# RMS norm with repeated rows: one store cut in two, and a load that waits for its first part

## The chip, the cores and the metric

The kernel runs on one core of a Trainium2 chip. The metric is the device time of one execution in microseconds (us); lower is better. Before the change it is 238.33 us, the median of 3 runs (238.19 to 238.34).

## The reference: what is computed

The input `x` has 8 x 512 rows of 2048 float32 values, `gamma` has 2048. Each row is divided by its root mean square, multiplied by `gamma`, and written twice, one copy after the other:

```python
x_rep = np.repeat(x, 2, axis=1)
rms = np.sqrt((x_rep ** 2).mean(axis=-1, keepdims=True) + 1e-6)
return ((x_rep / rms) * gamma[None, None, :]).astype(np.float32)
```

So 33.6 MB are read and 67.1 MB written. The arithmetic is done once for each input row, not once for each output row.

## The kernel before: tiles, stages and order

**The buffer.** One tile `y` fills most of the on-chip memory: 128 partitions, each with 24 rows of 2048 float32 (8 KB a row). The code names three groups of eight rows by their first row: `first` = 0, `second` = 8, `third` = 16. A load brings eight input rows to every partition (64 KB a partition, 8.39 MB in all). Four loads make the whole input, L0 to L3 here. Every load gives two stores, each of four input rows doubled to eight output rows, so also 64 KB a partition and 8.39 MB. There are eight stores, written here as S00 and S01 (from L0), S10 and S11 (from L1), and so on. In `out_t` a partition's 64 KB of a store are contiguous in device memory.

**Two groups.** The function `four(n, ...)` handles loads `n` and `n + 1` and their four stores, and is called with `n` = 0 and `n` = 2. Inside it:

- Load `n` goes to rows 4 to 11 (`first + K`), load `n + 1` to rows 16 to 23 (`third`).
- Rows 4 to 7 are normalised into rows 0, 2, 4, 6 and copied into 1, 3, 5, 7; these eight are store (n, 0).
- Rows 8 to 11 are normalised, last row first, into 14, 12, 10, 8, and copied to the odd rows; store (n, 1).
- Rows 16 to 19 go into rows 0 to 7, once store (n, 0) has read them: store (n + 1, 0).
- Rows 20 to 23 go into rows 16 to 23: store (n + 1, 1).

So L2, the first load of the second group, writes rows 4 to 11 and may start only when S01 (rows 8 to 15) and S10 (rows 0 to 7) have been read out. L3 writes rows 16 to 23 and waits for S11.

**The engines.** `squares` runs on ScalarE (ACT): a square with a sum for each row, then a square root over the sums. `scale` runs on VectorE (DVE): a reciprocal, then for each row one operation that multiplies by the reciprocal and by `gamma_b`. `repeat` makes the second copy of the rows, on ACT or DVE. The order on every engine is the order of the code (`manual_schedule`); waits are put in by the framework wherever two accesses touch the same bytes of `y`.

**The queues.** All loads and stores are issued by SyncE (SP) and go through one DMA queue, in order: L0, L1, S00, S01, S10, S11, L2, L3, S20, S21, S30, S31. Each is carried by 16 DMA engines, 8 partitions to an engine. SP waits in order too: while it waits to issue L2 it can't issue L3. `gamma` comes through ACT's DMA queue in `constants()`, one large DMA and `E` small ones of 16 values, into rows 0 to 2 of `y` on partition 0. GpSimd (POOL) then spreads them to all partitions in two `partition_broadcast` operations (L132 and L136). POOL does nothing else but four small fills at the start.

The lines that matter below are L50 (issue of a load), L53 (issue of a store), L63, L67 (`squares`), L73, L75 (`scale`), L82 (`repeat`), and L122 to L136 (`constants`).

Of the kernel before, what the change touches and what calls it, by code (L numbers as in the profile page):

```python
# [1 line left out]

# [4 lines left out]


@with_exitstack
def kernel(  # L10
    ctx: ExitStack,
    tc: tile.TileContext,
    x: bass.AP,
    gamma: bass.AP,
    out: bass.AP,
):
    nc = tc.nc
    P = nc.NUM_PARTITIONS
    f32 = mybir.dt.float32
    Act = mybir.ActivationFunctionType  # L20
    Alu = mybir.AluOpType

    B, S, D = x.shape
    Bo, So, Do = out.shape
    R = So // S
    assert R == 2 and D == Do and B == Bo and So == S * R
    eps = 1e-6
    inv_d = 1.0 / float(D)


    K = 4
    N = B * S
    ntiles = N // (P * K)
    assert N % (P * K) == 0 and ntiles == 8
    H = 2
    x_t = x.rearrange("b s d -> (b s) d").rearrange("(n p k) d -> n p k d", p=P, k=H * K)
    out_t = out.rearrange("b s d -> (b s) d").rearrange("(n p h j) d -> n h p (j d)", p=P, h=H, j=K * R)

    singles = ctx.enter_context(tc.tile_pool(name="singles", bufs=1))
    rows = ctx.enter_context(tc.tile_pool(name="rows", bufs=1))  # L40
    junk = ctx.enter_context(tc.tile_pool(name="junk", bufs=1, space=bass.MemoryType.PSUM))
    small = ctx.enter_context(tc.tile_pool(name="small", bufs=4))

    y = rows.tile([P, 3 * K * R, D], f32, name="y")
    first, second, third = 0, K * R, 2 * K * R

    def load(n, at):
        nc.sync.dma_start(out=y[:, at : at + H * K, :], in_=x_t[n])  # L50

    def store(n, h, to):
        nc.sync.dma_start(  # L53
            out=out_t[n, h], in_=y[:, to : to + K * R, :].rearrange("p j d -> p (j d)")
        )

    def squares(at, rows):

        n = len(rows)
        ss = small.tile([P, n], f32, name=f"ss{n}")  # L60
        for c, k in enumerate(rows):
            sq = junk.tile([P, D], f32, name="sq")
            nc.scalar.activation(  # L63
                out=sq[:], in_=y[:, at + k, :], func=Act.Square, accum_out=ss[:, c : c + 1]
            )
        rms = small.tile([P, n], f32, name=f"rms{n}")
        nc.scalar.activation(out=rms[:], in_=ss[:], func=Act.Sqrt, scale=inv_d, bias=eps_t[:])  # L67
        return rms

    def scale(at, to, rows, rms):  # L70
        n = len(rows)
        rstd = small.tile([P, n], f32, name=f"rstd{n}")
        nc.vector.reciprocal(out=rstd[:], in_=rms[:])  # L73
        for c, k in enumerate(rows):
            nc.vector.scalar_tensor_tensor(  # L75
                out=y[:, to + R * k, :], in0=y[:, at + k, :], scalar=rstd[:, c : c + 1],
                in1=gamma_b[:], op0=Alu.mult, op1=Alu.mult,
            )

    def repeat(to, k0, k1, copy):  # L80
        y_r = y[:, to + R * k0 : to + R * k1, :].rearrange("p (k r) d -> p k r d", r=R)
        copy(out=y_r[:, :, 1, :], in_=y_r[:, :, 0, :])  # L82

    ctx.enter_context(tc.manual_schedule())

    half = K // 2
    up, down = list(range(K)), list(range(K - 1, -1, -1))

    def four(n, constants, step):


        load(n, first + K)
        constants()
        load(n + 1, third)
        for rows in (up[:half], up[half:]):
            scale(first + K, first, rows, squares(first + K, rows))
        repeat(first, 0, half, nc.scalar.copy)
        repeat(first, half, K, nc.vector.tensor_copy)
        store(n, 0, first)
        scale(second, second, down, squares(second, down))  # L100
        repeat(second, half, K, nc.scalar.copy)
        for k in range(0, half, step):
            repeat(second, k, k + step, nc.vector.tensor_copy)
        store(n, 1, second)
        roots = [squares(third + h * K, up) for h in range(H)]
        scale(third, first, up, roots[0])
        repeat(first, 0, half, nc.scalar.copy)
        repeat(first, half, K, nc.scalar.copy)
        store(n + 1, 0, first)
        scale(third + K, third, up, roots[1])  # L110
        repeat(third, 0, K, nc.scalar.copy)
        store(n + 1, 1, third)

    gamma_b = singles.tile([P, D], f32, name="gamma_b")
    G, E = 16, 3
    C = D // G - E
    gamma_s = y[0:1, 0:2, :].rearrange("p k (c d) -> p (k c) d", c=G // 2)
    gamma_t = y[0:1, 2, :]
    eps_t = singles.tile([P, 1], f32, name="eps_t")

    def constants():
        nc.scalar.dma_start(  # L122
            out=gamma_s[0:1, :, :C],
            in_=gamma[: G * C].rearrange("(p c d) -> p c d", p=1, c=G),
        )
        for c in range(E):
            at = G * C + c * G
            nc.scalar.dma_start(
                out=gamma_t[0:1, c * G : (c + 1) * G],
                in_=gamma[at : at + G].partition_broadcast(1),  # L130
            )
        nc.gpsimd.partition_broadcast(  # L132
            out_ap=gamma_b[:, : G * C].rearrange("p (c d) -> p c d", c=G),
            in_ap=gamma_s[0:1, :, :C],
        )
        nc.gpsimd.partition_broadcast(out_ap=gamma_b[:, G * C :], in_ap=gamma_t[0:1, : E * G])  # L136
        nc.vector.memset(eps_t, eps)  # L137

        root = singles.tile([P, 1], f32, name="root")[:]
        nc.scalar.activation(out=root, in_=eps_t[:], func=Act.Sqrt)  # L140

    four(0, constants, half)
    four(2, lambda: None, 1)


# [1 line left out]
_INS = ['x', 'gamma']  # L147
_OUTS = [((8, 1024, 2048), 'float32')]


# [23 lines left out]
```

## Time and profile before

| | |
|---|---|
| median of 3 runs | 238.33 us |
| the profiled execution's own time | 238.07 us |
| its span (first to last instruction) | 236.2 us |
| DVE busy | 84.5 us (36%) |
| ACT busy | 110.2 us (47%) |
| POOL busy | 2.8 us (1%) |
| moved by DMA | 100.68 MB, 426 GB/s over the span |
| GpSimd's broadcast L132 starts, takes | 10.65, 2.24 us |
| GpSimd's broadcast L136 starts, takes | 23.01, 0.32 us |

The profile shows one execution. Times of single events count from the start of its span. An engine's busy time has no waiting in it. A DMA has two times: when its queue's engine issued it, and when it landed, that is when its completion was signalled. Between the two it can stand in the queue behind other transfers. The time outside the span (238.07 less 236.2) is the launch and the end of the program.

### The profile page before, as it was taken

To read this page: it belongs to the slowest core of one execution; us is meant where nothing else is said; L and a number is where in the kernel's file an instruction comes from. 1 tells how busy PE (TensorE), PEld (TensorE's weight loads), DVE (VectorE), ACT (ScalarE), POOL (GpSimd) and SP (SyncE) were. 2 spreads that over 40 slices of the span, in tenths; PEclk is the share of its full clock that TensorE was granted. 3 is DMA by queue.
4 is the path that set the end of the run, shared out by engine and by line. 5 is a ranking of instruction groups with operands and counts; after the bars stand their busy time and mean duration, and the time that the engine had idled before them with its cause. 6 is when DMAs were issued, how large, how long until landed. Compare 5 with 4: busy or idle time off the path is not lost.

```text
span 236.2 us, 226 instructions
## 1 busy us (share of the span) xinstructions
DVE 84.5 (36%) x48; ACT 110.2 (47%) x86; POOL 2.8 (1%) x6
## 2 busy tenths in 40 slices
DVE  0000396594699500000000007928919992000000
ACT  2001989479998470000000049991999957400000
POOL 0110000000000000000000000000000000000000
DMA  9898989989898989989898998989898998989894
GB/s 355 356 533 355 510 377 422 466 366 522 355 533 356 533 355 422 466 377 510 355 533 355 488 400 355 533 355 533 355 533 355 488 399 355 533 355 533 355 533 178
DMA packets 1767, 100.68 MB, mean 426 GB/s; under 512 B 230, under 2 KB 230, under 8 KB 230
## 3 DMA queue, kind: packets, MB, share of 16 engines
q1 hardware_dynamic: 1728, 100.66, 98.7%
q10 hardware_dynamic: 38, 0.01, 0.0%
q14 instruction: 1, 0.01, 0.0%
HBM read 33.56 MB, written 67.11 MB: 426 GB/s over the span
## 4 chain that ended last, share of the span: by engine, by line
DMA 45%; ACT 26%; DVE 12%; issue 2%; DVEq 0%
DMA y<-in_x_dram 26%; DMA out_dram<-y 20%; ACT sq L63 15%; DVE y L75 12%; ACT y L82 11%; ACT rms L67 1%; DVE rstd L73 0%; DVEq L75 0%
## 5 line engine op out<-in xcount | busy, mean ns | idle before, releaser
L63 ACT ACTIVATE sq<-y 128x2048 f32<-128x2048 f32 x32 | 60.1, 1878 | 71.1 <-DMA y<-in_x_dram 70.4
L75 DVE SCALAR_TENSOR_TENSOR y<-y,rstd,gamma_b 128x2048 f32<-128x2048 f32 x32 | 73.8, 2349 | 1.6 <-DMA out_dram<-y 1.0
L82 ACT COPY y<-y 128x4096 f32<-128x4096 f32 (+1 forms) x10 | 42.6, 4283 | 19.1 <-DVE y L75 18.3
L73 DVE RECIPROCAL rstd<-rms 128x4 f32<-128x4 f32 (+1 forms) x10 | 1.7, 170 | 109.2 <-ACT rms L67 109.2
L82 DVE COPY y<-y 128x4096 f32<-128x4096 f32 (+1 forms) x5 | 9.2, 1865 | 0.1
L63 ACT ACTIVATION_READ_ACCUMULATOR sq<-y 128x1 f32 x32 | 6.0, 186 | 0.0
L67 ACT ACTIVATE rms<-ss,eps_t 128x4 f32<-128x4 f32 (+1 forms) x10 | 3.0, 297 | 0.3
L140 ACT ACT_TABLE_LOAD x1 | 1.3, 1283 | 2.6 <-issue 2.6
L132 POOL PARTITION_BROADCAST gamma_b<-y x1 | 2.2, 2243 | 10.2 <-DMA y<-in_gamma_dram 10.2
L136 POOL PARTITION_BROADCAST gamma_b<-y x1 | 0.3, 323 | 10.1 <-DMA y<-in_gamma_dram 10.1
L137 DVE MEMSET eps_t<- 128x1 f32 x1 | 0.1, 59 | 0.8 <-PEq L158 0.8
L140 ACT ACTIVATE root<-eps_t 128x1 f32<-128x1 f32 x1 | 0.2, 203 | 0.0
L158 POOL MEMSET const-bfloat16-1.0<- 128x1 bf16 x1 | 0.1, 102 | 0.0
L158 POOL MEMSET const-float32-0.0<- 128x1 f32 x1 | 0.1, 99 | 0.2 <-issue 0.2
L158 POOL MEMSET const-uint8-127<- 128x1 uint8 x1 | 0.1, 101 | 0.0
L158 POOL MEMSET const-float32-1.0<- 128x1 f32 x1 | 0.1, 98 | 0.0
## 6 DMA issues: line engine op xcount, KB each, us to landing
out_dram<-y SPq DMA_DIRECT2D x8, 24.8
y<-in_x_dram SPq DMA_DIRECT2D x4, 31.4
y<-in_gamma_dram ACTq DMA_DIRECT2D x3, 0.1 KB
y<-in_gamma_dram ACTq DMA_DIRECT2D x1, 7.8 KB, 9.8
```

The costliest lines, as they stand in the source:

```text
L63: nc.scalar.activation(out=sq[:], in_=y[:, at + k, :], func=Act.Square, accum_out=ss[:, c : c + 1])
L67: nc.scalar.activation(out=rms[:], in_=ss[:], func=Act.Sqrt, scale=inv_d, bias=eps_t[:])
L73: nc.vector.reciprocal(out=rstd[:], in_=rms[:])
L75: nc.vector.scalar_tensor_tensor(out=y[:, to + R * k, :], in0=y[:, at + k, :], scalar=rstd[:, c : c + 1], in1=gamma_b[:], op0=Alu.mult, op ...
L82: copy(out=y_r[:, :, 1, :], in_=y_r[:, :, 0, :])
L132: nc.gpsimd.partition_broadcast(out_ap=gamma_b[:, : G * C].rearrange("p (c d) -> p c d", c=G), in_ap=gamma_s[0:1, :, :C],)
L136: nc.gpsimd.partition_broadcast(out_ap=gamma_b[:, G * C :], in_ap=gamma_t[0:1, : E * G])
L137: nc.vector.memset(eps_t, eps)
L140: nc.scalar.activation(out=root, in_=eps_t[:], func=Act.Sqrt)
L158: nc = _bacc.Bacc("TRN2", target_bir_lowering=False, num_devices=1)
```

## The change

Three edits. The last store of the first group, S11, is issued as two DMAs, one of seven rows of 8 KB in every partition and one of the eighth row. Between the two groups GpSimd copies one element, from row 4 to row 16 of partition 0. It writes a byte range that the seven-row DMA reads, so it waits for that DMA to land. It reads a byte range that L2 will write, so L2 waits for the copy. And `gamma` is cut differently: 2016 values in the large DMA and two small ones of 16 (before 2000 and three). A fourth, small edit: in the second group the two rows' copy on DVE before S21 is one operation and not two. The number of DMAs on both queues together stays 16.

```diff
-    def store(n, h, to):
-        nc.sync.dma_start(
-            out=out_t[n, h], in_=y[:, to : to + K * R, :].rearrange("p j d -> p (j d)")
-        )
+    def store(n, h, to, cuts=()):
+        rows = y[:, to : to + K * R, :].rearrange("p j d -> p (j d)")
+        ends = [c * D for c in (0, *cuts, K * R)]
+        for c0, c1 in zip(ends, ends[1:]):
+            nc.sync.dma_start(out=out_t[n, h][:, c0:c1], in_=rows[:, c0:c1])
...
-    def four(n, constants, step):
+    def four(n, constants, cuts=()):
...
-        for k in range(0, half, step):
-            repeat(second, k, k + step, nc.vector.tensor_copy)
+        repeat(second, 0, half, nc.vector.tensor_copy)
         store(n, 1, second)
...
-        store(n + 1, 1, third)
+        store(n + 1, 1, third, cuts)
...
-    G, E = 16, 3
+    G, E = 16, 2
...
-    four(0, constants, half)
-    four(2, lambda: None, 1)
+    four(0, constants, (K * R - 1,))
+    nc.gpsimd.tensor_copy(out=y[0:1, third, 0:1], in_=y[0:1, first + K, 0:1])
+    four(2, lambda: None)
```

In the built program the copy on GpSimd stands after its two broadcasts. Its own queue waits first for L0, then for L1 and the seven-row DMA, then for ACT. On SP the order becomes L0, L1, S00, S01, S10, S11's seven rows, S11's one row, L2 (which waits for S00, S01, S10 and the copy), L3 (which waits for both parts of S11), and the four stores of the second group.

## The prediction

> **What bounds the kernel now.** I read the page's busy times first, then its DMA queues.
>
> ```profile
> DVE 84.5 (36%) x48; ACT 110.2 (47%) x86; POOL 2.8 (1%) x6
> q1 hardware_dynamic: 1728, 100.66, 98.7%
> ```
>
> No engine is near its span. The one queue that carries all loads and stores keeps the 16 DMA engines busy for 98.7% of it. The kernel is a train of 12 equal transfers, and only what leaves a hole in that train or makes it longer costs time. The chain that ended last, in order of time, gives the train's marks (start, duration, what):
>
> ```profile
> 0.72 21.92 DMA y<-in_x_dram
> ...
> 76.17 23.86 DMA out_dram<-y
> 100.03 0.02 issue
> 100.04 38.78 DMA y<-in_x_dram
> 138.82 0.02 issue
> ...
> 155.30 22.23 DMA out_dram<-y
> ```
>
> Landings: L0 at 22.64, S10 at 100.03, L2 at 138.82, S20 at 177.53. From L0 to S10 there are four transfers, 77.39 us, 19.35 each. From L2 to S20 two, 38.71, again 19.35. From S10 to L2 two (S11 and L2), 38.79, so 0.09 more than 2 x 19.35: the hand-over from stores to loads costs about 0.09 today, with L2 queued long before. L0, which found idle engines, took 21.92 from issue to landing, 2.57 more than 19.35. These two numbers, 0.09 for a load already in the queue and 2.57 for a load that has to start the engines, are what the forecast turns on.
>
> The timeline around the change:
>
> ```profile
> 80.04 7.02 ACT L82 COPY y<-y 128x8192 f32<-128x8192 f32 x1 [3.90 <-DVE y L75]
> 87.08 0.33 SPq L53 DMA_DIRECT2D out_dram<-y  x1
> 100.04 20.04 SPq L50 DMA_DIRECT2D y<-in_x_dram  x2
> 138.85 1.88 ACT L63 ACTIVATE sq<-y 128x2048 f32<-128x2048 f32 x1 [51.79 <-DMA y<-in_x_dram]
> ```
>
> S11 is issued at 87.08 and lands at 119.73: the second L50 issue is released by it. L2 is issued at 100.04, so it stands in the queue for the whole 19 us of S11. No compute runs between 87.06 and 138.85; ACT and DVE wait for L2 and nothing else.
>
> **The change, part by part.**
>
> *The new wait, on the path.* L2's issue moves from 100.04 to after the seven rows' landing and the copy.
>
> 1. Seven rows land. S11 starts when S10 ends, landing to landing: 100.03 + 7/8 x 19.35 = 116.96.
> 2. GpSimd wakes. The same engine waited for small DMAs twice:
>
> ```profile
> 0.33 0.10 POOL L158 MEMSET const-uint8-127<- 128x1 uint8 x1
> 10.65 2.24 POOL L132 PARTITION_BROADCAST gamma_b<-y  x1 [10.22 <-DMA y<-in_gamma_dram]
> 23.01 0.32 POOL L136 PARTITION_BROADCAST gamma_b<-y  x1 [10.12 <-DMA y<-in_gamma_dram]
> ```
>
> The first followed its DMA's landing by 0.08 (landing 10.57 in the trace's records of completions). The second, which like the copy has a separate wait instruction ahead of it (43 ns on POOL's queue), followed by 0.18 (landing 22.83). I take 0.18, because the copy has two such waits, of which the second is the late one; 0.08 is the lower end.
> 3. The copy of one element. No such operation is in the trace. The fill of 128x1 takes 0.10 and reads nothing; the 48-column broadcast takes 0.32 and also moves data across partitions; the 2000-column one, 2.24, is the far upper bound. I take 0.20, between the two nearest; below nothing it can't go.
> 4. GpSimd's end to SP's issue. ACT's copy ends at 87.06 and SP issues at 87.08 (0.02); after DVE's copy before S00 it is 0.08. I take 0.05. L2 is then issued at 116.96 + 0.18 + 0.20 + 0.05 = 117.39, 17.35 later than today.
> 5. From issue to landing. If the engines have run out by the time its data come, the row is L0's, 21.92: landing at 139.31 against 138.82, **+0.49**. If the eighth row covers the start completely, L2 follows the train as it does today: +0.00, or -0.09 if the hand-over cost goes too. Which end is nearer? The eighth row is 1/8 x 19.35 = 2.42 of work; it starts on the engines when the seven rows end there, and the completion records of S10 come 0.44 after the last engine's final packet. So at 116.96 some 1.98 is left, and the engines are empty at 118.94. L2 is issued at 117.39, 1.55 before that. In L0's start the first packets began 1.02 to 1.51 after the issue and took 2.8 to 3.5 each instead of 2.42. Together L0's data come as if they started 1.6 to 2.2 after the issue, that is at 119.0 to 119.6 here. That is after 118.94, so I take the L0 row. Its spread, and an easier start in mid-run than at the program's beginning (ACT issues gamma beside L0), keep the lower end open.
>
> By the Trainium skill, "DMA: Bandwidth & Descriptors", section "Latency and other measured facts", a DMA issued from SP has its first byte after some 600 ns. By that L2's data would come at 117.99, before 118.94, and the sum would be +0.00, not +0.49. In L0's start the first packet began 1.02 us after the issue.
>
> *Who waits behind it.* On SP only L3 stands behind L2. Its other condition, S11's end, comes at about 119.4 to 119.7 as now; then it has the whole of L2, 19 us, to get into the queue. On POOL nothing follows the copy. On ACT, DVE everything after L2 shifts with it: S20's issue (155.30) stays 16.5 after L2's landing. L3 ends 19.35 after L2, at 158.17 today, so S20 is in the queue 2.9 ahead of need, and both shift alike. The later stores are earlier still: S30 is issued at 192.23, 4.6 before S21 lands. So a shift of L2 is passed on whole to the end, and nothing gives it back.
>
> *S11 in two DMAs.* One more issue on SP, 0.33, at 87.4: SP then waits for 30 us, so nothing. On each DMA engine 8 packets of 64 KB become 8 of 56 KB and 8 of 8 KB. The trace's packets of 500 B (gamma's large DMA) took 26 ns against 18 by the 64 KB rate, so about 8 ns a packet: 8 x 8 = 0.06 in the worst case. It lies under the restart if there is one (the eighth row then ends later, before L2's data), else it adds 0.06. Taken: 0.
>
> *Gamma.* One 0.2 us issue less on ACT before its table load, 16 more columns in the first broadcast (2.24 x 2016/2000, +0.02), 16 fewer in the second. POOL has the last piece some 4.8 earlier than 23.01, since each small DMA waits its turn between two 64 KB packets on one engine. DVE first needs `gamma_b` at 27.34, after ACT's squares of L0. So 0; even 4 us later it would be the first store's 2.8 us of slack (issued at 39.20, L1 landing at 42.0) that pays. The upper bound of a gain is the small packets' own time on one engine, under 0.05.
>
> *One copy for two on DVE before S21.* The two take 2.36 together, a 128x4096 one 2.29: 0.07 off S21's issue at 172.0, which waits in the queue until S20 ends at 177.5. Hidden by 5 us: 0.
>
> *Sum:* +0.49 on the profiled execution's 238.07 gives 238.56. The median shown is 0.26 above that execution; on it the sum is 238.82, **238.8 us** (+0.2%). 0.2% (0.48 us) is about what a measurement of this kernel can tell from no change; my likeliest value stands on that border.
>
> **The rivals.**
>
> A. *The engines run dry and L2 restarts them* (likeliest, 0.62). By the ends of steps 2 to 4 (0.08 to 0.18, 0.10 to 0.32, 0.02 to 0.08) and an issue-to-landing between 21.4 (19.35 + 1.6 + 0.44) and 22.0 (with 2.2): L2 lands between 138.82, where B begins, and 139.54, so 238.4 to 239.1.
>
> B. *The eighth row covers the restart* (0.20), the rival on the other side: not slower. Place: the 16 engines' queues at about 118.9. It decides if L2's data can start within 1.55 of the issue, or if GpSimd's two steps take 0.1 in place of 0.38. For it: the queue is still running, not cold, and the first packet of L0 began after 1.02. Against it: those first packets took up to 1.1 longer than the others. Time: 238.2 to 238.4.
>
> C. *GpSimd's copy is slow to start* (0.10). It is its first copy, after 94 us without work. Every microsecond goes to the end in full. If it takes as long as the 2.24 broadcast, +0.49 + 2.04: 240.9; half of that, 239.9. Against it: the fills at 0.24 took 0.10 at once. The Trainium skill, "GPSIMD Engine Reference", section 2.1 "Instruction dispatch", puts some 6 us on the first call of freshly loaded code, which would give 244.6 if it were met here. No row of this trace shows such a wait.
>
> D. *Rows of 8 KB are stored at a poor rate, or the loads start slowly after a full stop of the writes* (0.05). The eighth row at half the rate: 2.4 more, of which 0.5 lies under the restart, so 240.2. Against it: the 500 B packets already ran at 0.7 of the rate.
>
> E. *Gain* (0.03): the 0.09 hand-over goes, or the packets run better after the engines are in step. No hole in the train is there to close, so it can't reach 0.2% by any row I have; 238.2.
>
> **How the numbers follow.** Predicted is A's value, 238.8, rounded. Slower by over 0.2% is A's upper part (two thirds of 0.62, since copy and start are more likely to be longer than taken than shorter), with C and D: 0.41 + 0.15 = 0.56, and 0.01 of what I can't name. Within 0.2%: A's lower part, B and most of E: 0.40. Faster: 0.03. The range reaches from B's low end with the 0.1 by which the three runs differ, 238.1, over A to C's half case, 239.8; what is left out is half of C, most of D and a little of E.
>
> **What would show it.** Right: L2's issue near 117.4, its landing near 139.3, about 21.9 between; the chain has a GpSimd copy and SP's issue between S11 and L2; the queue's share falls by about 0.2%; DVE and ACT as before. B: L2 lands at 138.7 to 138.9 for an issue at 117.4. C: a long copy or a late issue. D: S11's second part lands after 119.8. Wrong altogether would be a time under 237.9: then the train itself ran faster, and the rate of 19.35 is not the limit I take it for.

## The result, and the profile after

The changed kernel takes 238.92 us (median of 9 runs, 238.66 to 239.12) against 238.26 for the kernel before (median of 9, 238.04 to 238.43). The ratio is 1.0028, with a 95% interval from 1.0018 to 1.0038: slower by about 0.66 us. The profiled execution after is one of 238.92 with a span of 237.1; the one before had 238.07 and 236.2.

The busy times and the load queue on the page of the changed kernel:

```profile
DVE 84.4 (36%) x47; ACT 110.2 (46%) x86; POOL 2.9 (1%) x7
q1 hardware_dynamic: 1872, 100.66, 98.6%
```

No engine works longer than before, but for GpSimd's 0.1. The queue has 144 packets more (the split store: 128 of data and 16 completions), and its share falls from 98.7 to 98.6% of a span that is 0.8 longer.

The chain that ended last, changed kernel, in order of time (start, duration, what):

```profile
87.19 29.76 DMA out_dram<-y
116.95 0.03 POOLq L143
116.97 0.08 issue
117.05 0.19 POOLq L170
117.25 0.02 issue
117.27 22.18 DMA y<-in_x_dram
139.44 0.02 issue
...
155.99 22.37 DMA out_dram<-y
178.36 0.03 issue
```

Before, this chain went from S10 (landed 100.03) straight into L2 (issued 100.04, landed 138.82). Now it follows the seven rows of S11 to 116.95, GpSimd's queue (the line L170 is its drain, which stands over the copy's own time), SP's issue at 117.27, and L2, which lands at 139.44. S20 lands at 178.36 (before 177.53).

The same place in the timeline:

```profile
87.19 1.62 SPq L56 DMA_DIRECT2D out_dram<-y  x2
117.06 0.17 POOL L143 COPY y<-y 1x1 f32<-1x1 f32 x1 [96.31 <-DMA out_dram<-y]
117.27 2.57 SPq L50 DMA_DIRECT2D y<-in_x_dram  x2
```

The copy starts 0.11 after the landing and takes 0.17; SP issues L2 0.03 after its end. The first line also shows something not foreseen: the two issues of S11 together take 1.62, since the second, for the one row, took 1.24 on SP and not 0.33. SP has nothing else to do then.

And SP's waits:

```profile
SPq L50 <- POOL y L143: 17.1, 1, 17.1
SPq L50 <- DMA out_dram<-y: 13.0, 2, 11.2
```

L2's issue now waits 17.1 us for GpSimd, after it had waited for S10.

**What L2's start cost.** From S10's landing to L2's is 39.38 us in the changed kernel, 38.79 before: 0.59 more. The trace's records of single packets say how. They name no engine, but a packet's start can be matched with the end of the one before it. After the one row 15 of the 16 DMA engines went on to L2 without a pause and one stood idle for 0.41, 0.02 us on average, so L2 had come into the queue just in time. But the first L2 packets took 0.03 to 1.14 longer than 2.42, 0.57 on the average of 16 engines with the few slow second ones counted. Before, at the same hand-over, the last packets of S11 were drawn out by 0.17 on average.

### The profile page after: what moved, and what is told of

Read it like the earlier page. It is cut to its first block, busy times and chain, and to the rows that moved or that the text cites. A ratio compares the mean times of both kernels' runs of the same rounds, so it can differ in the third digit from the quotient of the medians.

```text
span 237.1 us, 231 instructions
## 1 busy us (share of the span) xinstructions
DVE 84.4 (36%) x47; ACT 110.2 (46%) x86; POOL 2.9 (1%) x7
## 3 DMA queue, kind: packets, MB, share of 16 engines
q1 hardware_dynamic: 1872, 100.66, 98.6%
## 4 chain that ended last, share of the span: by engine, by line
DMA 50%; DVE 21%; ACT 13%; issue 2%; POOLq 0%; DVEq 0%; SPq 0%
DMA out_dram<-y 31%; DVE y L76 20%; DMA y<-in_x_dram 19%; ACT y L83 7%; ACT sq L64 5%; DVE y L83 1%; DVE rstd L74 0%; ACT rms L68 0%; POOLq L170 0%; DVEq L76 0%; POOLq L143 0%; SPq L56 0%
## 5 line engine op out<-in xcount | busy, mean ns | idle before, releaser
L83 DVE COPY y<-y 128x4096 f32<-128x4096 f32 x4 | 9.2, 2294 | 0.1
L143 POOL COPY y<-y 1x1 f32<-1x1 f32 x1 | 0.2, 173 | 96.3 <-DMA out_dram<-y 96.3
```

What stands on the lines that cost most here:

```text
L143: nc.gpsimd.tensor_copy(out=y[0:1, third, 0:1], in_=y[0:1, first + K, 0:1])
```

## The experiments

Theory 1: the loss is L2's late issue; after the one row the DMA engines start anew on L2. Theory 2: the loss is the split store itself (8 KB packets, or its slow second issue). Theory 3: it is in the gamma or DVE edit. Each kernel ran beside the kernel before on the same chip, and differences are between the medians there.

**Only the split, and only the other edits; more cover, and none.** The first:

```diff
-    nc.gpsimd.tensor_copy(out=y[0:1, third, 0:1], in_=y[0:1, first + K, 0:1])
```

> The changed kernel without the copy on GpSimd: S11 in two DMAs, gamma in three DMAs and one copy on DVE stay, L2 waits only for S10 and stands in the queue as before. Theory 1 (all of the loss is the late issue of L2, after which the DMA engines run dry and start again): the time of the kernel before, 238.3, and L2 lands at 138.8. Theory 2 (the loss is the split store, by its 8 KB packets or its slow second issue): about 238.9, and S11's one row lands later than 119.8. Theory 3 (the loss is in the gamma or DVE edit): about 238.9, with L0 or the first store later.

Measured: 238.70 against 238.11, 0.59 slower, where theory 1 had none. Yet L2 behaved as theory 1 says. Its chain:

```profile
76.11 23.78 DMA out_dram<-y
...
99.97 38.75 DMA y<-in_x_dram
...
155.19 22.60 DMA out_dram<-y
```

L2 lands at 138.72, as early as before. So the split alone does not move L2, and the loss of this kernel lies elsewhere: S20 lands 39.07 after L2 (before 38.71), and 2.16 to 2.24 us of each execution lie outside the span (before 1.79 to 1.87). The one row landed at 119.62, before the 119.8 of theory 2; in the changed kernel its eight packets of 8 KB on an engine took 0.31 each, 2.47 together, where one of 64 KB takes 2.42.

The second, on the kernel before:

```diff
-    G, E = 16, 3
+    G, E = 16, 2
...
-    four(2, lambda: None, 1)
+    four(2, lambda: None, half)
```

> The kernel before with only the gamma cut (two small DMAs, not three) and the single copy on DVE. Theories 1 and 2: 238.3, no change. Theory 3: 238.9.

Measured: 238.77 against 238.11, 0.66 slower, as theory 3 expected, and with neither the split nor the wait. Without the split these two edits lose as much as with it, so nothing of theory 2 is seen. Its one profile is of its slowest execution (241.2, where the other eleven took 238.69 to 239.05) and is not read here. Outside the span lie again 2.14 to 2.25.

The third, on the changed kernel:

```diff
-    four(0, constants, (K * R - 1,))
+    four(0, constants, (K * R - 2,))
```

> The changed kernel with S11 cut into six rows and two, so that the load waits for six. By the train's step the six rows land at 114.5, L2 is issued at 114.9 and two rows, 4.8 us of work, are left on the engines less the 0.4 of the landing. Theory 1: the start of L2 (1.6 to 2.2 us from issue to data) is covered with 2 us to spare, L2 lands at 138.8 to 138.9 and the time is that of before, 238.3. Theory 2: still 238.9, since the store is still split and the copy still there. If the copy's wait costs by itself, whatever lies in the queue: also 238.9.

Measured: 238.54 against 238.11, 0.43 slower. The chain:

```profile
114.90 23.98 DMA y<-in_x_dram
...
155.42 22.44 DMA out_dram<-y
```

L2 is issued at 114.90 and lands at 138.87: its start is covered, as expected. The time did not come back as expected: S20 lands 38.99 after L2, and 1.91 to 2.00 lie outside the span.

The fourth, on the kernel before:

```diff
+    nc.gpsimd.tensor_copy(out=y[0:1, third, 0:1], in_=y[0:1, first + K, 0:1])
     four(2, lambda: None, 1)
```

> The kernel before (S11 whole, gamma in four DMAs) with the copy on GpSimd, which now waits for all of S11. Theory 1: S11 lands at 119.7, L2 is issued at 120.0 and lands 22.0 to 22.2 later, at 142.1; that is 3.3 later than before and 2.7 later than in the changed kernel, so 241.6. Theory 2: with no split there is no loss beyond the wait's own 0.3, 238.6.

Measured: 241.07 against 238.11, 2.96 slower (expected 3.3). The chain:

```profile
87.21 32.17 DMA out_dram<-y
...
119.70 21.73 DMA y<-in_x_dram
```

With no cover at all L2 is issued at 119.70, lands 21.73 later at 141.43, and 41.34 after S10. The DMA engines now stand idle for 2.24 on average, and L2's first packets again take 0.61 longer.

So L2's place follows the wait in the three whose profile is read, but two kernels with L2 in its old place are also slower. The gamma and DVE edits do something of their own.

**What the small edits do.** The packet records show one more kind of DMA: a packet of 8 KB, 0.31 us, on a queue named "instruction". I took it for a refill of one engine's stream of instructions; the runs below bear this out, since its place moves with the number of instructions on ACT. In the kernel before it falls at 75.0; the DMA queues in the window from 70 to 78 us:

```profile
q14 instruction: 1, 0.01, 0.2%
```

In the changed kernel it falls at 153.2 and is in the window from 150 to 156:

```profile
q14 instruction: 1, 0.01, 0.3%
```

Theory 4: what matters is that place. At 118, where stores give way to loads, the 16 DMA engines fall into step again (first to last completion 0.62 us before it, 0.33 after), so an early delay of one engine vanishes there and a late one stays. Four kernels tell these apart. The changed kernel with gamma's four DMAs:

```diff
-    G, E = 16, 2
+    G, E = 16, 3
```

> The changed kernel with gamma in four DMAs as before: the split store, the copy and the new wait stay. A new theory 4 stands beside theory 1: the instruction stream of one engine is refilled by an 8 KB DMA (its own queue, 0.31 us, one packet) which in the kernel before falls at 75 us, ahead of the hand-over from stores to loads at 118, where the DMA engines fall into step again and early engines wait anyway; in all kernels with the new gamma cut it falls at 152 to 153, after the hand-over, delays one DMA engine by 0.3 for the rest of the run, and that is in the time. Theory 1 alone: 238.1 + 0.6 to 0.8 = 238.8, as the changed kernel. Theory 4 with a restart of about 0.5: the refill is back at 75 and the time is 238.1 + 0.5 = 238.6, about 0.25 below the changed kernel. Theory 4 alone: 238.1.

Measured: 239.04 against 238.20, 0.84 slower; the interval of the ratio, 1.0018 to 1.0043, overlaps with the changed kernel's. The refill is back at 75.0, and the time did not fall. So the gamma edit is not what makes the changed kernel slow. In its trace:

```profile
117.24 21.98 DMA y<-in_x_dram
...
155.76 22.84 DMA out_dram<-y
```

L2 lands 39.20 after S10 (0.41 more than before) and S20 39.39 after L2 (0.68 more): six last packets of L3 were drawn out, by up to 0.7. Why is not known.

The kernel before with only the gamma edit:

```diff
-    G, E = 16, 3
+    G, E = 16, 2
```

> The kernel before with the gamma cut alone (two small DMAs, not three; the two copies on DVE stay two). Theory 4, if the stream is that of ACT, which issues gamma's DMAs: the refill at 152 and 238.6 to 238.8, as with both edits (238.77). If the stream is another engine's: refill at 75, 238.1.

Measured: 238.46 against 238.20; ratio 1.0009, interval 1.0001 to 1.0018. The refill is at 152.6. L2 lands as before (38.81 after S10), S20 0.26 later after L2 (38.97). Outside the span lie 1.79 to 1.88, as before. The packet records show what the refill did here. It stands between two load packets of one DMA engine, and the load packet behind it took 2.70 where the others took 2.42. From the end of L3 on this engine is the last of the 16: at the end it is done 0.27 after the next one, and the other 15 are done at 234.99, where all 16 were done at 235.00 in the kernel before. So in this execution the end is late by the refill alone. And the stream is one that loses instructions with a gamma DMA less, which is ACT's.

The kernel before with only the single copy on DVE:

```diff
-    four(2, lambda: None, 1)
+    four(2, lambda: None, half)
```

> The kernel before with the one copy on DVE alone (gamma in four DMAs). Theory 4 with ACT's stream: refill at 75, 238.1. With DVE's stream: refill at 152, 238.6 to 238.8.

Measured: 238.60 against 238.20; ratio 1.0009, interval 0.9999 to 1.0018. The refill stays at 75.1 and the median span is that of before, 236.4. What is longer is the time outside the span, 2.15 to 2.25. This was not expected by any theory.

The changed kernel with ACT's stream moved on:

```diff
-        nc.scalar.activation(out=root, in_=eps_t[:], func=Act.Sqrt)
+        for _ in range(25):
+            nc.scalar.activation(out=root, in_=eps_t[:], func=Act.Sqrt)
```

> The changed kernel with 24 more square roots of one value on ACT at the start, where ACT waits for L0 until 22.7 (24 x 0.2 = 4.9 us, hidden). They move ACT's stream on by 24 instructions. Theory 4 with ACT's stream: the refill moves from 153 back to somewhere between 55 and 90, ahead of the hand-over, and the time falls by 0.2 to 0.3 to about 238.6, the rest being the restart. Theory 1 alone, or a stream of another engine: refill at 153 and 238.8 to 238.9.

Measured: 238.80 against 238.20, 0.60 slower. The refill is at 41. S20 lands 38.70 after L2, as in the kernel before, and not 38.92; the time is little better, 0.60 slower where the changed kernel was 0.66, which these intervals can't tell apart. L2 lands 39.34 after S10: the restart is there unchanged.

**Dose and cover.** The last kernels cross the wait's length with the rows that cover it, all with gamma in four DMAs. Six rows and two:

```diff
-    G, E = 16, 2
+    G, E = 16, 3
...
-    four(0, constants, (K * R - 1,))
+    four(0, constants, (K * R - 2,))
```

> The changed kernel with two things undone in size: S11 cut into six rows and two, and gamma in four DMAs. Theory 1 with theory 4 (the restart costs, and by itself the place of the refill does): L2 is issued at 114.8, lands at 138.8, the refill is at 75, the span is that of before, 236.2 to 236.4, and the time 238.2 to 238.4. If the split store or the copy cost anything besides the restart, 238.5 and more.

Measured: 238.57 against 238.11, 0.46 slower. L2 as expected:

```profile
114.62 0.03 POOLq L143
...
114.94 23.85 DMA y<-in_x_dram
```

It lands at 138.79, 38.68 after S10. The span did not come back in full: 236.65 in the median (236.3 before), and another 0.12 lies outside it. S20 is 0.25 late after L2, with the refill at 74.9, so in this kernel the refill can't be its cause.

Seven rows and one, with a long copy:

```diff
-    G, E = 16, 2
+    G, E = 16, 3
...
-    nc.gpsimd.tensor_copy(out=y[0:1, third, 0:1], in_=y[0:1, first + K, 0:1])
+    nc.gpsimd.tensor_copy(out=y[0:1, third, 0:1024], in_=y[0:1, first + K, 0:1024])
```

> Seven rows and one, gamma in four DMAs, and GpSimd's copy made of 1024 elements on the one partition, not one. From the broadcasts (0.31 us for 32 columns, 2.26 for 2016, so about 1 ns a column) the copy should take 1.1 to 1.3 us, 1.0 more than with one element. Theory 1: this comes out in full, 239.04 + 1.0 = 240.0. If the loss does not come from L2's late issue: 239.0.

Measured: 239.80 against 238.11, 1.69 slower. The timeline:

```profile
116.95 1.03 POOL L143 COPY y<-y 1x1024 f32<-1x1024 f32 x1 [93.76 <-DMA out_dram<-y]
118.00 1.68 SPq L50 DMA_DIRECT2D y<-in_x_dram  x2
```

The copy took 1.03, 0.86 more than with one element, and the loss grew by 0.85 (from 0.84 to 1.69). L2 lands 40.33 after S10, in its one trace 1.13 later than with the short copy.

The same copy with six rows and two, the further edit to that kernel:

```diff
-    four(0, constants, (K * R - 1,))
+    four(0, constants, (K * R - 2,))
```

> The same copy of 1024 elements, with six rows and two. L2 is issued at about 115.8 and its data come by 117.4 to 118.0, before the engines are through with S11 at 118.9. Theory 1: the long copy is hidden, as in the run with six rows and the short copy, 238.2 to 238.4. If a wait on GpSimd's copy costs its own length wherever it stands: 239.3.

```profile
114.76 1.03 POOL L143 COPY y<-y 1x1024 f32<-1x1024 f32 x1 [91.35 <-DMA out_dram<-y]
115.82 4.08 SPq L50 DMA_DIRECT2D y<-in_x_dram  x2
```

Measured: 238.62 against 238.11, 0.51 slower, where the short copy had 0.46. With seven rows the same 0.86 came out in full in the medians, with six they show nothing of it, as far as the intervals (1.0005 to 1.0033 here, 1.0012 to 1.0030 with the short copy) can tell. In this trace, though, L2 lands 39.09 after S10, 0.41 later than with the short copy: the first packets were slow again, by 0.35 on the same average. The step after it was shorter than with the short copy (38.69 and 38.96). So at an issue of 115.8 the start is no longer fully covered, though no DMA engine stood idle.

The kernel before with the gamma edit, and ACT's stream moved on by the same 24 square roots:

```diff
-    G, E = 16, 3
+    G, E = 16, 2
...
-        nc.scalar.activation(out=root, in_=eps_t[:], func=Act.Sqrt)
+        for _ in range(25):
+            nc.scalar.activation(out=root, in_=eps_t[:], func=Act.Sqrt)
```

> The kernel before with gamma in three DMAs, which alone read 238.46 with the refill at 152.6, and 24 more square roots of one value on ACT at the start. Theory 4 with ACT's stream: the refill moves to about 41, ahead of the hand-over, and the time goes back to 238.2. If the gamma cut costs by something else (its own transfers): still 238.45.

Measured: 238.36 against 238.11, ratio 1.0013, interval 1.0004 to 1.0021; without the extra square roots it was 1.0009. So theory 4 is not borne out in the time. The refill did move, to 41.7, and S20 did land 38.68 after L2 again. But in this profile 0.45 had been lost already before S10 (landing at 100.48). The fastest of its executions took 238.08 (before 237.99), the fastest with the refill at 152.6 took 238.36. For the time that points to theory 4 and does not settle it; what the refill costs in one execution is seen in the packet records of the kernel with gamma's edit alone.

All of them together, but for the kernel with both small edits, whose one profile is of its slowest execution. "Two steps" are the times between landings, S10 to L2 and L2 to S20, from the profiled execution; "loss" is the median less that of the kernel before on the same chip:

| kernel | rows of S11, small gamma DMAs | refill at | L2 issued | S10 to L2 | L2 to S20 | outside the span | loss |
|---|---|---|---|---|---|---|---|
| before | 8, 3 | 75.0 | 100.04 | 38.79 | 38.71 | 1.8 | |
| after | 7+1, 2 | 153.2 | 117.27 | 39.38 | 38.92 | 1.8 | 0.66 |
| split only | 7+1, 2 | 152.6 | 99.97 | 38.83 | 39.07 | 2.2 | 0.59 |
| gamma's edit alone | 8, 2 | 152.6 | 100.06 | 38.81 | 38.97 | 1.8 | 0.26 |
| one DVE copy only | 8, 3 | 75.1 | 100.18 | 38.73 | 38.69 | 2.2 | 0.40 |
| gamma, with square roots | 8, 2 | 41.7 | 100.56 | 38.75 | 38.68 | 1.8 | 0.25 |
| after, gamma undone | 7+1, 3 | 75.0 | 117.24 | 39.20 | 39.39 | 1.8 | 0.84 |
| after, with square roots | 7+1, 2 | 41.2 | 117.41 | 39.34 | 38.70 | 1.8 | 0.60 |
| six rows | 6+2, 2 | 152.7 | 114.90 | 38.79 | 38.99 | 1.95 | 0.43 |
| six rows, gamma undone | 6+2, 3 | 74.9 | 114.94 | 38.68 | 38.96 | 1.95 | 0.46 |
| six rows, long copy | 6+2, 3 | 75.1 | 115.82 | 39.09 | 38.69 | 1.95 | 0.51 |
| seven rows, long copy | 7+1, 3 | 74.9 | 118.00 | 40.33 | 38.71 | 1.8 | 1.69 |
| wait for all of S11 | 8, 3 | 75.1 | 119.70 | 41.34 | 39.15 | 1.95 | 2.96 |

The step from S10 to L2 goes with L2's issue alone: 38.7 to 38.8 for any issue up to 114.9, 39.1 at 115.8, 39.2 to 39.4 at 117.2 to 117.4, 40.33 at 118.00 and 41.34 at 119.70. From 117.2 on L2 lands 21.7 to 22.3 after its issue, as L0 did (21.92). No other edit touches it. The step from L2 to S20 and the time outside the span move by 0.2 to 0.4 with edits that the prediction took for nothing.

## Why the prediction was right, and where it was not

The forecast was 238.8, slower by 0.2%; measured were 238.92 and 0.28%. The place of the likeliest case, A, was right: the loss that carried the forecast is at L2's start. Its picture was half right (step 5), and two terms that were put at nothing were not nothing. So it is in part luck that 238.8 stands only 0.12 from the measured time. The profiled execution after is 0.85 longer than the one before, not 0.49; the medians differ by 0.66, from 238.26 and not from 238.33.

- **Step 1, the seven rows' landing.** 116.96 forecast, 116.95 measured.
- **Steps 2 to 4, the chain over GpSimd.** 0.18 + 0.20 + 0.05 forecast; 0.11 + 0.17 + 0.03 measured. L2 was issued at 117.27, not 117.39. Rival C, a slow first copy, did not occur: GpSimd's first copy, 96.3 us after its last work, took 0.17.
- **Step 5, issue to landing.** 21.92 forecast from L0's row, 22.18 measured. The landing, 139.44, was forecast at 139.31. So the term that carried the sum (+0.49) measured +0.62 against the profile before, of which 0.03 came from ahead of S10. The picture behind it was only half right: 15 of the 16 engines did not run dry, L2's packets were there in time, but the first ones were slow by 0.57 on average. Slow first packets are in the forecast's term, since L0's row has them; the runs show that they come even where an engine goes on without a pause. So rival B's condition was in the main met, and L2 was late all the same. That the eighth row covers the issue is not enough, it has to cover the slow first packets too. With two rows and the short copy that is so (S10 to L2 as before), which is why rival B was wrong by a row.
- **The skill's first byte.** By the Trainium skill, "DMA: Bandwidth & Descriptors", section "Latency and other measured facts", L2's first byte was due 0.6 us after its issue. No run here shows a packet so early: the first of L2 began 1.0 us after the issue, and where the engines stood idle, in the kernel that waits for all of S11, the 16 began 0.97 to 1.91 after it. The measured 1.0 decides; for 15 of 16 engines here it was still in time. It doesn't follow that the start is then free; the slow packets were the cost.
- **Rival D.** Not met: the one row landed at 119.43, before the 119.8 that would have shown it. Its price didn't follow from its own terms: 2.4 more, 0.5 of it under the restart, is 1.9 on top of 238.8, so 240.7 and not 240.2.
- **"A shift of L2 is passed on whole".** Right in kind: +0.62 at L2's landing, +0.83 at S20's, +0.84 in the span. The extra 0.2 comes in between L2 and S20, where the refill falls and where one last packet of L3 was drawn out by 0.31. The engine with the refill and the engine with that packet are done within 0.01 of each other at the end, so either alone would have ended this execution at the same time.
- **"Gamma: 0" and "One copy for two on DVE: 0".** These are the steps that failed. Alone, gamma's edit cost 0.26, without touching L2 or any wait that I had looked at; in its profiled execution that is the refill on one DMA engine. The copy's edit cost 0.40 in the median, with an interval that just reaches no change; the time outside the span was 2.15 to 2.25 in each of its executions, against 1.78 to 1.87. My search for cover was right: nobody waited for them. What I had not priced is that an instruction more or less moves a refill, and that the time outside the span goes with it. Together, without the split and the wait, they cost 0.66, the sum of the two. In the changed kernel they don't add up in that way: with gamma undone the loss was 0.84, not less, and the time outside the span is 1.79 to 1.87, as before. GpSimd had the last piece of gamma 2.57 earlier (its second broadcast starts at 20.44), not 4.8; nothing waited for it.
- **The likely size of the restart in the time.** With seven rows the loss is 0.60 to 0.84 in three kernels, with six 0.43 to 0.51 in three. The three with six rows all have 0.12 more outside the span, which the three with seven don't; in spans alone the losses are 0.6 to 0.8 and 0.3 to 0.4 (medians against those of the kernel before beside them, for the five run with it). So 0.2 to 0.5 us of the loss is the uncovered start, and about 0.3 stays with six rows. It has no single cause.

In the packet records that 0.3 is a wider spread of the 16 DMA engines at the end. The first engine is done at 234.6 to 234.7 in every kernel that has L2 issued by 115.8. The last is done at 235.0 to 235.1 in the kernel before and in the one with DVE's edit alone, and at 235.2 to 235.5 in the others. What made the last one late differs between the profiled executions. With only the split, and with six rows, it is the engine with the refill, last by 0.23. With six rows and gamma undone, four last packets of L3 were drawn out, by up to 0.32. With six rows and the long copy it is L2's own start. What stays open is why L3's last packets are drawn out in some kernels, and how often each of these happens: there is one profile for each kernel.

No kernel here beats the one before.

## What to carry to other kernels

Where one queue is busy for 99% of the span, a new wait ahead of a transfer has to be covered twice: for the way from the awaited landing to the next issue (here 0.32), and for the start of the transfer after the issue, slow first packets included. Here the first DMA engine was through with the queued work 1.0 us after the issue with seven rows, which left 0.59 to pay; 2.7 with six rows and the long copy, which left 0.3; and 3.7 with six rows and the short copy, which left nothing. When the effect sought is a few tenths of a microsecond, edits that only change the number of instructions have to be run alone, since they can cost as much as the change itself.

## What the runs showed that was not expected

- A refill of an instruction stream is an 8 KB packet of 0.31 us on one of the 16 DMA engines that carry the loads. It moved from 75 to 152 or 153 us with one DMA issue less on ACT, and to 41 with 24 small operations more. With the refill at 152 to 153, L2 to S20 took 0.2 to 0.36 longer in four of four kernels. In the slowest execution of the kernel with both small edits it fell at 154.7, on an engine that was not the last, and the step was 38.68. With it at 41 or 75, the step took no longer in five kernels after the one before, and 0.25 to 0.68 longer in three. The load packet behind the refill took 0.28 longer at 152 to 153, and 0.11 to 0.13 at 41 or 75. The Trainium skill, "Runtime: NRT & Kernel Launch", section "Instruction fetch mechanics", calls such fetches mostly hidden, and names blocks of 16 KiB; the packet here has 8 KB, and it was hidden only in some of its places.
- The time outside the span goes with the number of DVE's instructions in the trace, waits included: with 62 (before, after and five more) it is 1.78 to 1.89, with 61 (three kernels) 2.14 to 2.25, with 63 (four) 1.91 to 2.01. What causes this was not tried.
- The second of two stores issued back to back took 1.24 us on SP and not 0.33, in the changed kernel, and 1.20 to 1.26 in every other kernel with the split store. Nothing waited for it.
- Sixteen DMA engines that have drifted apart by 0.62 us come back to 0.33 where stores give way to loads that already stand in the queue: the early engines' last store packets were drawn out by up to 0.65.
